# Layer A of a hybrid decoder trunk in the tokens' own order, with the convolved tiles of TensorE alone turned to phase order and back

## The chip, the cores and the metric

The kernel runs on one core of a Trainium2 chip. The metric is the device time of one execution in microseconds (us), the median of several runs. The engines are TensorE (PE: matmul and transpose), VectorE (DVE), ScalarE (ACT), GpSimd (POOL, hardly used here) and SyncE (SP, which issues all DMAs in one queue).

## What is computed

A trunk of two layers over x of 1024 tokens by 1024 channels, in float32. Layer A is a Conformer convolution, layer B a differential attention. The change touches layer A:

```
h = rms_norm(x, g_pre);  u = h @ w_in            # 1024 x 3072
a, b, z = split(u, 3)
c = a * sigmoid(b)
c = causal_depthwise_conv(c, w_dw) + b_dw        # 31 taps along the tokens
c = silu(layer_norm(c, ln_g, ln_b))              # over the channels
y = (c * silu(z)) @ w_out
x = x + rms_norm(y, g_post)
```

Layer B then computes K and V from x, eight heads of attention with two softmaxes each, a gated projection and a last normalised sum.

## The kernel before, in words

Everything is held with channels on the 128 partitions and tokens along the free dimension: 8 channel tiles c of 128, and 2 halves t of 512 tokens. Every matmul is done as three products of high and low fp32r parts (`THREE`), so each weight tile and each activation tile is split into a high part (a cast on ACT) and a low part (a subtraction on DVE): `wprep` for weights, `split` for activations. The activations of layer A's matmuls are `act[0]` and `act[1]`, one for each half.

The program is not in its written order. `Plan` collects operations with their data dependences, `schedule` simulates the engines with fixed costs and orders the operations by priorities, and `emit` writes the result out as a fixed order for each engine. The priorities come from the constants in `TUNE` and from an offset for each label in `OFFSETS`. On the chip each engine takes its instructions in that order and waits for data or for a buffer to come free. A `gate` binds only the plan's order.

Layer A before works in **phase order**: position s * 128 + n holds token 8 * n + s. The input is loaded in that order from a second copy of x, `xP`, that the host prepares. A "half" t of layer A's first part is then four phases, not 512 tokens that follow each other.

- `ab` (L835) computes, for a half and a channel tile, b and a: the product `pb_` times the RMS factor `rn[t]`, a tanh on ACT, then (tanh + 1) * `pa_` and a second DVE product with the RMS factor. For channel tiles of odd number the result goes to `cc` in phase order, contiguous (L858). For those of `DVC` = 0, 2, 4, 6 it is written in token order, with a stride of 8 elements (L847 to L855, two DVE instructions for each half).
- `conv` (L863) convolves. For tiles of `DVC`, 31 taps on DVE over 1024 tokens, the last of them reading with a stride of 8 so that `cb[t]` gets phase order (L873 to L879). For odd tiles, on TensorE: `cc` goes to DRAM, comes back as `xq` with 16 channels by 8 phases on the partitions, 80 matmuls follow, ACT adds the bias into `yq`, eight DMAs write `cv_d`, and two DMAs bring the result to `cb[0]` and `cb[1]` (L905).
- `zproj` (L916) projects z: 16 tiles of 24 matmuls each, for c = 0 to 4 both halves, then 5 to 7 of half 0 and of half 1. Its evacuations multiply by `rn[t]` and take SiLU into `sz[t]`. The buffers of `sz` take the space of the convolution's buffers (`wc`, `cc`, `xq`, `yq`, `ya`), so no `sz` is written before the last convolution is through with them.
- `lnorm` (L946) subtracts the mean, sums squares and spreads 1/std over the partitions by a matmul into a `pjB` PSUM tile. `rstd_bc` then copies that tile into `rn[t]`, the buffer that held the RMS factor of half t (L955). Then, for each c and each t: times 1/std, SiLU on ACT, times `sz`. A second loop (L966) splits to `act[t]`, which is wanted in token order: each half of tokens takes its elements from both `cb[0]` and `cb[1]`, with two casts on ACT and two subtractions on DVE of 128x256 for each tile, strided.
- `ymm` (L982) projects to y, 8 tiles of 24 matmuls for each half, which read `act[t]` from k = 0 to 7. `ypost` (L997) normalises, adds x and splits again for layer B.

PSUM: `pj` and `pjA` with 2 tiles each take the projections, `pjB` with 2 tiles the TensorE convolution, the means, the spread factors and half of y's tiles.

Of the kernel before, what the change touches and what calls it, by code (L numbers as in the profile page):

```python
# [13 lines left out]
ALU = mybir.AluOpType  # L14
# [4 lines left out]
P = 128  # L19
S = 1024  # L20
D = 1024
# [109 lines left out]
class Op:  # L131
# [16 lines left out]
TUNE = dict(LOOK=3.8682, BG=694967571912821345177968431443880025688058404755344259219980288,  # L148
           FS=45301, FS0=1201, CS=0, EV=157158, WT=0.6301, CV0=46679, CV1=113660, WP=2955,
           ZS=-61794, PT0=8, PT1=8)  # L150

OFFSETS = {"": 24050, "w": -5958, "start1": -20454, "x0": -59, "x1": -2750, "x2": 2563, "x3":
# [417 lines left out]
def trunk(ctx: ExitStack, tc, xT, xP, wC, prm, wA, wAo, wK, wV, wB, wBo, wBo2, gpost, outT, out2):  # L570
# [208 lines left out]
    def start_first():  # L779
# [3 lines left out]
        def load(k):  # L783
            R.dma(xh(k), xP[k * P : (k + 1) * P, :TH], 4 * P * TH)
# [33 lines left out]
    def start_second():  # L818
# [3 lines left out]
        for k in range(NT):  # L822
            R.dma(xh(k), xP[k * P : (k + 1) * P, TH:], 4 * P * TH)
# [638 lines left out]
```

## Time and profile before

| what | value |
|---|---|
| median of 3 runs | 1139.7 us (1139.49 to 1141.55) |
| the profiled execution's own time | 1131.87 us |
| its span, first to last instruction | 1130.0 us |
| mean granted TensorE clock | 0.984 |
| PE busy | 1070.5 us (95% of the span) |
| DVE busy | 918.9 us (81%) |
| ACT busy | 442.7 us (39%) |
| DMA | 121.31 MB, mean 107 GB/s |

The profile shows one execution, with every instruction's start and duration. It is read in three ways below: busy time of each engine in a stretch of the span, the waits of an engine with what ended them, and single instructions in order of time. The profiled execution is 7.8 us shorter than the median of the timed runs.

### The profile page before, as it was taken

Reading aid. Unit: us, or ns where it says so; the run is one execution under the profiler, and the core shown is the slowest. Engines: PE = TensorE matmul, PEld = TensorE weight load, DVE = VectorE, ACT = ScalarE, POOL = GpSimd, SP = SyncE. Lnnn points to the kernel's source line nnn. Section 1 sums busy time; section 2 is a strip of 40 time slices with the busy share of each in tenths; the row PEclk is TensorE's granted clock in tenths of the full one; section 3 lists DMA queues with packets and bytes.
Section 4 is the critical chain, followed back from the end, with each engine's and each line's share of the span. In section 5 each row is a group of like instructions: output and inputs, shape, how many; then the busy total and the mean of one; then the engine's idle time right before and its main releaser. Section 6 shows DMA issues by size and latency. Waiting matters only on the chain.

```text
span 1130.0 us, 15409 instructions
## 1 busy us (share of the span) xinstructions
PE 1070.5 (95%) x5790; PEld 877.1 (78%) x5790; DVE 918.9 (81%) x1828; ACT 442.7 (39%) x832; POOL 4.7 (0%) x19
## 2 busy tenths in 40 slices
PE   6999999999985999989999999999999999989896
PEld 4777878787863787877788877988779888767785
DVE  7999999999759379957878878788697877888657
ACT  8111020214356446434445334443344443455421
POOL 0000000000000000000000000000000000000000
PEclk9999999999996999999999999999999999999999
DMA  9121652523101245452013221141212311632564
GB/s 341 59 75 38 206 168 75 168 75 75 38 19 56 76 148 187 141 187 83 20 56 129 96 68 46 57 150 57 75 38 75 114 56 56 219 110 82 176 241 160
DMA packets 52985, 121.31 MB, mean 107 GB/s; under 512 B 5552, under 2 KB 22192, under 8 KB 51760
## 3 DMA queue, kind: packets, MB, share of 16 engines
q1 hardware_dynamic: 52912, 120.34, 31.2%
q8 instruction: 45, 0.74, 0.3%
q14 instruction: 28, 0.23, 0.1%
HBM read 90.96 MB, written 29.36 MB: 106 GB/s over the span
## 4 chain that ended last, share of the span: by engine, by line
PE 52%; DVE 9%; DMA 4%; issue 1%; ACT 1%; SPq 0%; DVEq 0%; ACTq 0%
PE pj L499 34%; PE o L499 6%; PE s L1171 5%; PE t L1223 3%; PE pjB L499 2%; DVE big L540 1%; DVE whl L540 1%; PE t L499 1%; DVE sm L540 1%; DMA outT<-tmp 1%; DMA wraw<-wBo 1%; PE pjA L499 1%; DMA x1t_d<-xr 1%; DMA tmp<-x_d 1%; DMA wraw<-wK 0%
## 5 line engine op out<-in xcount | busy, mean ns | idle before, releaser
L499 PE MATMUL pj<-act,whl 128*128 128x512 f32 x1968 | 532.1, 403 | 19.4 <-ACT whl L533 5.7
L499 PEld LDWEIGHTS pj<-act,whl 128*128 128x128 f32 x1968 | 354.9, 190 | 100.7 <-DVE act L540 7.3
L499 PE MATMUL pjA<-act,whl 128*128 128x512 f32 x672 | 183.7, 399 | 2.2 <-DVE sz L540 1.2
L499 PEld LDWEIGHTS pjA<-act,whl 128*128 128x128 f32 x672 | 125.0, 188 | 33.9 <-DVE sz L540 1.7
L560 DVE SCALAR_TENSOR_TENSOR ya<-cc,pr,ya 128x1024 f32<-128x1024 f32 x116 | 148.6, 1281 | 2.7
L522 ACT ACTIVATE e<-e,sm 128x128 f32<-128x128 f32 (+7 forms) x128 | 99.2, 776 | 91.5 <-DVE sm L1180 47.7
L533 ACT CAST whl<-wraw 128x1024 fp32r<-128x1024 f32 (+1 forms) x84 | 85.9, 1027 | 101.3 <-PE pj L499 71.3
L540 DVE TENSOR_TENSOR whl<-wraw,whl 128x1024 fp32r<-128x1024 f32 (+1 forms) x84 | 99.9, 1194 | 14.7 <-ACT whl L533 14.6
L499 PE MATMUL pj<-whl,act 128*128 128x256 f32 x768 | 111.4, 284 | 0.5 <-DVE tmp L560 0.4
L499 PEld LDWEIGHTS pj<-whl,act 128*128 128x128 f32 x768 | 99.6, 188 | 3.6 <-DVE tmp L560 1.1
L499 PE MATMUL o<-at,vt 128*128 128x256 f32 x480 | 100.2, 299 | 2.3 <-DVE at L540 1.7
L1180 DVE CUSTOM_DVE_ANT_0 e<-s,dist 128x128 f32<-128x128 f32 (+7 forms) x128 | 94.5, 752 | 6.5 <-PE s L1171 4.3
L499 PEld LDWEIGHTS o<-at,vt 128*128 128x128 f32 x480 | 78.1, 189 | 16.9 <-issue 3.0
L540 DVE TENSOR_TENSOR at<-t,at 128x512 fp32r<-128x512 f32 (+1 forms) x80 | 50.7, 634 | 29.1 <-ACT at L533 28.6
L1171 PE MATMUL s<-ks,qs 64*128 64x512 f32 (+2 forms) x576 | 72.6, 372 | 0.3 <-DVE sm L1180 0.3
L533 ACT CAST at<-t 128x512 fp32r<-128x512 f32 (+1 forms) x80 | 43.4, 542 | 70.2 <-PE t L1223 69.1
L1171 PEld LDWEIGHTS s<-ks,qs 64*128 64x128 f32 x576 | 48.1, 187 | 20.7 <-issue 8.4
L499 PE MATMUL pjB<-act,whl 128*128 128x512 f32 x192 | 52.9, 404 | 11.3 <-ACT act L533 8.3
L560 DVE SCALAR_TENSOR_TENSOR e<-e,sm,e 128x128 f32<-128x128 f32 (+3 forms) x64 | 52.2, 817 | 1.5
L499 PEld LDWEIGHTS pjB<-act,whl 128*128 128x128 f32 x192 | 36.7, 192 | 21.0 <-ACT act L533 8.7
L1223 PE MATMUL t<-ident,e 128*128 128x128 f32 x288 | 50.5, 275 | 0.8 <-DVE og L540 0.8
L540 DVE TENSOR_TENSOR tmp<-pj,rn 128x512 f32<-128x512 f32 x48 | 32.7, 685 | 14.3 <-PE pj L499 9.2
(176 smaller groups left out, 1093.2 us busy)
## 6 DMA issues: line engine op xcount, KB each, us to landing
wraw<-wA SPq DMA_DIRECT2D x22, 512.0 KB, 3.5
wc<-wC SPq DMA_DIRECT2D x8, 1280.0 KB, 7.9
wraw<-wAo SPq DMA_DIRECT2D x16, 512.0 KB, 3.5
wraw<-wB SPq DMA_DIRECT2D x16, 512.0 KB, 3.4
v_d<-tmp SPq DMA_DIRECT2D x32, 256.0 KB, 2.5
vt<-v_d SPq DMA_DIRECT2D x16, 512.0 KB, 3.7
wraw<-wBo SPq DMA_DIRECT2D x16, 512.0 KB, 3.9
go_d<-fx SPq DMA_DIRECT2D x12, 512.0 KB, 2.6
```

Source lines behind the costliest of these rows:

```text
L499: e.matmul(w[0], lhsT=r[2 * i], rhs=r[2 * i + 1], start=start and i == 0, stop=stop and i == k - 1)
L522: e.activation(w[0], r[0], func, **kw)
L533: (e.copy if hasattr(e, "activation") else e.tensor_copy)(w[0], r[0])
L540: lambda e, r, w: e.tensor_tensor(w[0], r[0], r[1], alu), [a, b], [out])
L560: e.scalar_tensor_tensor(w[0], r[0], s if imm else r[2], r[1], o1, o2)
L1171: en.matmul(w_[2 * (m // 6) + m % 2], lhsT=r[2 * m], rhs=r[2 * m + 1], start=m % 6 < 2, stop=m % 6 >= 4)
L1180: en.tensor_tensor_reduce(w_[0], r[0], r[1], -(0.5 ** (h + 1)), 3e38, ALU.add, ALU.min, w_[1])
L1223: R.op([("PE", 110.0)], lambda en, r, w: en.transpose(w[0], r[0], ident), [aw[qq][:, k0 : k0 + P]], [t_ps[:, i, :]])
```

## The change

- x is loaded from `xT` in token order; `xP` is gone. A half is now 512 tokens that follow each other, all through layer A.
- `ab` multiplies (tanh + 1) by the RMS factor first, SBUF by SBUF, and then by `pa_`. For tiles of `DVC` the second product is written contiguously. For odd tiles it reads both operands with a stride of 8 elements and writes phase order for TensorE.
- `conv`: the last DVE tap is a plain instruction for each half. For odd tiles one DMA brings the whole convolved tile to a buffer `yb` (in the slots of `xq`), and two ScalarE copies of 128x512, reading with a stride, turn it to token order in `cb[0]` and `cb[1]`.
- `lnorm`: 1/std of half t goes to a `msum` buffer and no longer to `rn[t]`. The loop runs over half 0 with all its channel tiles and then over half 1, and each tile is split at once by `split`, one cast and one subtraction of 128x512, contiguous.
- The constants of the plan (`LOOK`, `BG`, `WT`) and all its offsets are new, so the written order of the whole kernel is redrawn. The code of layer B is the same.

```
-TUNE = dict(LOOK=3.8682, BG=694967571912821345177968431443880025688058404755344259219980288,
-           FS=45301, FS0=1201, CS=0, EV=157158, WT=0.6301, CV0=46679, CV1=113660, WP=2955,
+TUNE = dict(LOOK=2.2803,
+           BG=19323277573972505648901158565292249389628248258332383962132468097051787264,
+           FS=45301, FS0=1201, CS=0, EV=157158, WT=0.8342, CV0=46679, CV1=113660, WP=2955,
            ZS=-61794, PT0=8, PT1=8)
...
-            R.dma(xh(k), xP[k * P : (k + 1) * P, :TH], 4 * P * TH)
+            R.dma(xh(k), xT[k * P : (k + 1) * P, :TH], 4 * P * TH)
...
         pa_ = R.tile("pjA", TH)
         proj(pa_.all(), ha, act[t])
+        R.stt(sg.all(), sg.all(), 1.0, rb.all(), ALU.add, ALU.mult)
         if c in DVC:
-            o = cc[:, 32:].rearrange("p (n s) -> p s n", s=PH)._then(
-                lambda ap: ap[:, PH // 2 * t : PH // 2 * (t + 1)])
-            ph = "p (s n) -> p s n"
-            R.op([("DVE", 700.0)], lambda e, r, w: e.scalar_tensor_tensor(
-                w[0], r[0], 1.0, r[1], ALU.add, ALU.mult),
-                [sg.all().rearrange(ph, s=PH // 2), pa_.all().rearrange(ph, s=PH // 2)], [o])
-            if rb is not None:
-                R.op([("DVE", 700.0)], lambda e, r, w: e.tensor_tensor(
-                    w[0], r[0], r[1], ALU.mult), [o, rb.all().rearrange(ph, s=PH // 2)], [o])
+            R.tt(cc[:, 32 + t * TH : 32 + (t + 1) * TH], sg.all(), pa_.all(), ALU.mult)
             return
-        o = cc[:, t * TH : (t + 1) * TH]
-        R.stt(o, sg.all(), 1.0, pa_.all(), ALU.add, ALU.mult)
-        if rb is not None:
-            R.tt(o, o, rb.all(), ALU.mult)
+        ph = lambda v: v.all().rearrange("p (n s) -> p s n", s=PH)
+        o = cc[:, :S].rearrange("p (s n) -> p s n", s=PH)._then(
+            lambda ap: ap[:, :, P // 2 * t : P // 2 * (t + 1)])
+        R.op([("DVE", 1200.0)], lambda e, r, w: e.tensor_tensor(w[0], r[0], r[1], ALU.mult),
+             [ph(sg), ph(pa_)], [o])
...
             for t in range(2):
-                nat = lambda v: v.rearrange("p (n s) -> p s n", s=PH)._then(
-                    lambda ap, t=t: ap[:, PH // 2 * t : PH // 2 * (t + 1)])
-                R.op([("DVE", 720.0)], lambda e, r, w: e.scalar_tensor_tensor(
-                    w[0], r[0], r[2], r[1], ALU.mult, ALU.add),
-                    [nat(src(KW - 1)), nat(y.all()), tap(KW - 1)],
-                    [cb[t][:, c, :].rearrange("p (s n) -> p s n", s=PH // 2)])
+                R.stt(cb[t][:, c, :], src(KW - 1, t), tap(KW - 1),
+                      y[:, t * TH : (t + 1) * TH], ALU.mult, ALU.add)
...
+        yb = R.tile("xq", S, lane="Y")
+        R.dma(yb.all(), cv_d[c], 4 * P * S)
         for t in range(2):
-            R.dma(cb[t][:, c, :], cv_d[c, :, t * TH : (t + 1) * TH], 4 * P * TH)
+            src = yb.all().rearrange("p (s n) -> p n s", s=PH)._then(
+                lambda ap, t=t: ap[:, P // 2 * t : P // 2 * (t + 1)])
+            R.copy(cb[t][:, c, :].rearrange("p (n s) -> p n s", s=PH), src).alts = [("ACT", 1000.0)]
...
-            rb[t] = rstd_bc(sq_sum(t, lambda k: cb[t][:, k, :]), "dg0", "pjB", rn[t])
-        for c in range(NT):
-            for t in range(2):
+            rb[t] = rstd_bc(sq_sum(t, lambda k: cb[t][:, k, :]), "dg0", "pjB",
+                            R.tile("msum", TH))
+        for t in range(2):
+            for c in range(NT):
                 R.label = f"ln{t}{c}"
...
                 R.act(v, v, AF.Silu, scale=col(C_LNG, c), bias=col(C_LNB, c))
                 R.tt(v, v, sz[t][:, c, :], ALU.mult)
-
-        for t in range(2):
-            for c in range(NT):
                 R.label = f"sp{t}{c}"
-                for x in range(2):
-                    dst = act[t][:, c, x, :].rearrange("p (n s) -> p s n", s=PH)
...
+                split(act[t], c, v)
```

## Rows read from the trace of the kernel before

**Rows 1.** The view of windows, one row for each stretch of the span. Columns: the stretch and its length in us; busy time and, in brackets, instructions of PE, PEld, DVE, ACT and POOL; the granted TensorE clock (1.00 is 2.4 GHz); the DMA engines' mean busy share; GB/s.

```profile
0.00:28.00 28.00, 18.91 (x72) 13.88 (x73) 21.52 (x37) 22.93 (x39) 1.15 (x12) 1.00 0.92 343
28.00:262.00 234.00, 226.66 (x1134) 186.76 (x1132) 229.12 (x247) 38.19 (x69) 0.63 (x5) 1.00 0.34 109
...
289.00:325.00 36.00, 36.00 (x159) 29.08 (x158) 19.60 (x41) 11.27 (x18) 0.00 (x0) 1.00 0.09 30
325.00:335.00 10.00, 9.79 (x42) 7.54 (x41) 9.26 (x15) 9.77 (x17) 0.00 (x0) 1.00 0.00 0
335.00:360.00 25.00, 8.71 (x19) 5.80 (x20) 24.23 (x41) 19.53 (x34) 0.00 (x0) 0.66 0.21 63
...
440.00:520.00 80.00, 72.56 (x421) 60.41 (x420) 59.51 (x129) 31.66 (x58) 2.95 (x2) 0.98 0.43 144
520.00:1000.00 480.00, 477.24 (x2912) 396.30 (x2911) 387.29 (x956) 208.93 (x438) 0.00 (x0) 1.00 0.24 84
1000.00:1130.00 130.00, 114.89 (x584) 93.04 (x582) 92.77 (x240) 47.72 (x85) 0.00 (x0) 0.95 0.43 150
```

**Rows 2.** The view of waits for TensorE between 330 and 370 us: engine and line that waited, what ended the wait, total us, how often, the longest.

```profile
PE pjB L499 <- ACT act L533: 8.3, 1, 8.3
PE pj L499 <- DVE act L540: 5.6, 2, 5.1
PE pjB L499 <- DVE act L540: 3.0, 1, 3.0
```

**Rows 3.** The timeline of TensorE from 334 to 361 us (start, us, what, how many, and in square brackets the idle time before with what ended it): the end of the last tile of z and the first matmul of y.

```profile
333.69 1.09 PE L499 MATMUL pj<-act,whl 128*128 128x512 f32 x4
343.07 0.80 PE L499 MATMUL pjB<-act,whl 128*128 128x512 f32 x1 [8.29 <-ACT act L533]
```

**Rows 4.** The chain of waits, one piece of TensorE at full clock in y's stage.

```profile
390.55 4.20 PE pj L499 x18
```

**Rows 5.** The timeline of TensorE from 286 to 312 us: the two matmul pairs that spread 1/std over the partitions (the first for half 0, the second for half 1).

```profile
287.85 0.62 PE L499 MATMUL pjB<-dg,ones_r 128*128 128x512 f32 x2
...
310.37 0.62 PE L499 MATMUL pjB<-dg,ones_r 128*128 128x512 f32 x2
```

**Rows 6.** The timeline of VectorE from 318 to 326 us: z's evacuations and the first product with 1/std.

```profile
318.72 0.69 DVE L540 TENSOR_TENSOR sz<-pjA,rn 128x512 f32<-128x512 f32 x1 [6.78 <-PE pjA L499]
322.92 0.69 DVE L540 TENSOR_TENSOR sz<-pj,rn 128x512 f32<-128x512 f32 x1 [3.51 <-PE pj L499]
323.62 0.69 DVE L540 TENSOR_TENSOR sz<-pjA,rn 128x512 f32<-128x512 f32 x1
324.97 1.30 DVE L540 TENSOR_TENSOR big<-big,rn 128x512 f32<-128x512 f32 x2 [0.65 <-ACT rn L533]
```

**Rows 7.** The timeline of ScalarE from 322 to 326 us: the copy of 1/std of half 0 into `rn`.

```profile
324.35 0.59 ACT L533 COPY rn<-pjB 128x512 f32<-128x512 f32 x1
```

**Rows 8.** Groups of instructions by line and form between 320 and 372 us (count, then busy us and mean ns of one, then idle time before): the LayerNorm's products, SiLU and split.

```profile
L540 DVE TENSOR_TENSOR act<-big,act 128x256 fp32r<-128x256 f32 x32 | 18.5, 651 | 0.0
L533 ACT CAST act<-big 128x256 fp32r<-128x256 f32 x32 | 18.2, 698 | 6.7 <-DVE big L540 6.7
L522 ACT ACTIVATE big<-big,pr 128x512 f32<-128x512 f32 x16 | 12.3, 800 | 2.9 <-DVE big L540 2.9
L540 DVE TENSOR_TENSOR big<-big,sz 128x512 f32<-128x512 f32 x16 | 10.9, 690 | 1.1 <-ACT big L522 0.7 <-ACT sz L522 0.3
L540 DVE TENSOR_TENSOR big<-big,rn 128x512 f32<-128x512 f32 x16 | 10.7, 689 | 0.7 <-ACT rn L533 0.7
```

**Rows 9.** The same view from 0 to 400 us: `ab`'s products (strided at L854 and L850, contiguous at L540 and L560), the last tap (L876) and a contiguous product with a column scalar.

```profile
L560 DVE SCALAR_TENSOR_TENSOR act<-big,pr,act 128x512 fp32r<-128x512 f32 x16 | 11.5, 741 | 5.3 <-ACT act L522 5.3
...
L854 DVE TENSOR_TENSOR cc<-cc,rn 128x512 f32<-128x512 f32 x8 | 10.1, 1268 | 0.2
...
L876 DVE SCALAR_TENSOR_TENSOR big<-cc,pr,ya 128x512 f32<-128x512 f32 x8 | 9.9, 1270 | 0.1
L850 DVE SCALAR_TENSOR_TENSOR cc<-tmp,pjA 128x512 f32<-128x512 f32 x8 | 9.4, 1169 | 0.7 <-ACT tmp L522 0.7
...
L540 DVE TENSOR_TENSOR cc<-cc,rn 128x512 f32<-128x512 f32 x8 | 5.5, 681 | 0.0
L560 DVE SCALAR_TENSOR_TENSOR cc<-tmp,pjA 128x512 f32<-128x512 f32 x8 | 5.4, 677 | 0.0
```

**Rows 10.** The view of waits for TensorE between 28 and 262 us.

```profile
PE pj L499 <- DVE tmp L540: 5.0, 3, 2.5
PE pjA L499 <- DVE cc L850: 0.9, 1, 0.9
```

**Rows 11.** The timeline of all engines from 222 to 286 us: the last convolved tile of TensorE on its way to `cb`, and TensorE's wait behind it.

```profile
251.21 2.26 ACT L522 ACTIVATE yq<-pjB,pr 128x128 f32<-128x128 f32 x8 [19.97 <-PE pjB L499]
...
253.50 3.63 SPq L565 DMA_DIRECT2D cv_d<-yq  x8
...
257.29 1.92 SPq L565 DMA_DIRECT2D big<-cv_d  x2
...
262.62 1.67 PE L499 MATMUL pjA<-act,whl 128*128 128x512 f32 x6 [1.24 <-DVE sz L540]
```

**Rows 12.** The groups of ScalarE between 28 and 262 us: the weights' casts and `ab`'s tanh.

```profile
L533 ACT CAST whl<-wraw 128x1024 fp32r<-128x1024 f32 x18 | 18.8, 1049 | 58.7 <-PE pj L499 43.3 <-PE pjA L499 8.4 <-issue 7.1
L522 ACT ACTIVATE tmp<-tmp 128x512 f32<-128x512 f32 x16 | 10.1, 633 | 57.8 <-DVE tmp L540 57.8
```

More of the change, by code (lines that the diff above doesn't have):

```diff
@@ L144 @@
            ("SP", "POOL"): 940.0, ("SP", "SP"): 1000.0}
-TUNE = dict(LOOK=3.8682, BG=694967571912821345177968431443880025688058404755344259219980288,
-           FS=45301, FS0=1201, CS=0, EV=157158, WT=0.6301, CV0=46679, CV1=113660, WP=2955,
+TUNE = dict(LOOK=2.2803,
+           BG=19323277573972505648901158565292249389628248258332383962132468097051787264,
+           FS=45301, FS0=1201, CS=0, EV=157158, WT=0.8342, CV0=46679, CV1=113660, WP=2955,
            ZS=-61794, PT0=8, PT1=8)
-OFFSETS = {"": 24050, "w": -5958, "start1": -20454, "x0": -59, "x1": -2750, "x2": 2563, "x3":
[57 rows of a table removed]
+OFFSETS = {"": 20890, "w": 8673, "start1": -150, "x0": 332, "x1": 403, "x2": 60, "x3": 48533,
[55 rows of a table added]
 class Clock:
@@ L569, in trunk @@
 @with_exitstack
-def trunk(ctx: ExitStack, tc, xT, xP, wC, prm, wA, wAo, wK, wV, wB, wBo, wBo2, gpost, outT, out2):
+def trunk(ctx: ExitStack, tc, xT, wC, prm, wA, wAo, wK, wV, wB, wBo, wBo2, gpost, outT, out2):
     nc = tc.nc
@@ L822, in start_second @@
         for k in range(NT):
-            R.dma(xh(k), xP[k * P : (k + 1) * P, TH:], 4 * P * TH)
+            R.dma(xh(k), xT[k * P : (k + 1) * P, TH:], 4 * P * TH)
         for k in range(NT):
@@ L867, in conv @@
             tap = lambda j: col(C_TAP, (KW + 1) * DVC.index(c) + j)
-            src = lambda j: cc[:, 2 + j : 2 + j + S]
+            src = lambda j, t=None: (cc[:, 2 + j : 2 + j + S] if t is None else
+                                     cc[:, 2 + j + t * TH : 2 + j + (t + 1) * TH])
             y = R.tile("ya", S)
@@ L964, in lnorm @@
                 R.tt(v, v, sz[t][:, c, :], ALU.mult)
-        for t in range(2):
-            for c in range(NT):
                 R.label = f"sp{t}{c}"
-                for x in range(2):
-                    dst = act[t][:, c, x, :].rearrange("p (n s) -> p s n", s=PH)
-                    for u in range(2):
-                        src = cb[u][:, c, :].rearrange("p (s n) -> p s n", s=PH // 2)._then(
-                            lambda ap, t=t: ap[:, :, 64 * t : 64 * t + 64])
-                        d = dst._then(lambda ap, u=u: ap[:, 4 * u : 4 * u + 4])
-                        if x == 0:
-                            R.copy(d, src).alts = [("ACT", 306.0)]
-                        else:
-                            hi = f(act[t][:, c, 0, :]).rearrange("p (n s) -> p s n", s=PH)._then(
-                                lambda ap, u=u: ap[:, 4 * u : 4 * u + 4])
-                            R.tt(d, src, hi, ALU.subtract).alts = [("DVE", 336.0)]
+                split(act[t], c, v)
     def ymm(t):
@@ L1436 @@
         "xT": np.ascontiguousarray(np.asarray(x)[0].T),
-        "xP": np.ascontiguousarray(
-            np.asarray(x)[0].T.reshape(D, S // PH, PH).transpose(0, 2, 1).reshape(D, S)),
         "wC": np.ascontiguousarray(wc.reshape(NT * (NT // GB), P, GB * SH * P)),
```

112 rows, old and new, of the table OFFSETS are left out of this document.

## The prediction

> **What bounds the kernel now.** I read the windows by stage first [rows 1]. TensorE is busy in 95% of the span, and the reader should look for where it is not. From 520 to 1000 us, the attention, it misses 2.8 of 480 us; from 28 to 262, the projections and convolutions of layer A, 7.3 of 234; from 440 to 520, the passage to layer B, 7.4; at the two ends 9.1 and 15.1. One place stands out: from 335 to 360 us only 19 matmuls touch a stretch of 25 us, with the granted clock down to 0.66 as a mean of its two levels, while VectorE is busy for 24.2 of them and ScalarE for 19.5. Next I asked what TensorE waits for there: `act`, first its cast, then its subtractions [rows 2]. The timeline shows z's last matmuls at 333.7 to 334.8 and y's first at 343.07 after 8.29 us of nothing [rows 3]. So the LayerNorm between z and y bounds this stage, and TensorE bounds nearly everything else. The other stretch to read is 28 to 262, where VectorE is busy for 229.1 of 234 us: there the two engines are close to a tie.
>
> Why is the LayerNorm late? Its factor 1/std for half 0 was spread into PSUM at 287.85 [rows 5], but the first product with it starts at 324.97 [rows 6]. In between stands the copy of that factor into `rn[0]`, at 324.35 [rows 7]. `rn[0]` still held the RMS factor that z's evacuations of half 0 read, and the last of those starts at 323.62 [rows 6]. For 36 us the factor lay ready behind a buffer. VectorE was meanwhile busy for 19.6 of the 36 us from 289 to 325, ScalarE for 11.3 [rows 1]. Then both halves came at once, and `act[0]` needs elements of both, so TensorE had to wait for nearly all of it.
>
> **Term 1, the hole after z.** The change puts 1/std into a `msum` buffer whose last reader is the mean's matmul, and splits half 0 from half 0 alone. Half 0 then costs VectorE 8 x (0.69 + 0.69) for the two products and 8 x 0.68 for a contiguous subtraction, 16.5 us, and ScalarE 8 x 0.80 for SiLU and 8 x 0.59 for the cast, 11.1 us [rows 7 to 9]. Idle time before 325 is 16.4 us on VectorE and 24.7 on ScalarE [rows 1], and the ten us to 335 were already spent on this work. The last tile needs the z evacuated at 323.62; with SiLU of it (0.63, as for the tanh of the same form [rows 12]), product, cast and subtraction (0.69, 0.59, 0.68) it is ready near 327, and y reads it last of eight. So y can start when z ends. What comes back is 25.0 us less the time of 19 matmuls at the full rate of 4.20 / 18 = 0.233 us [rows 4], 4.4 us: 20.6, and 0.2 from 325 to 335 [rows 1]. **-20.8 us.** Next in line is half 1: another 16.5 us of VectorE under the 8 x 24 x 0.233 = 45 us that y's half 0 takes, so nothing is late there. The split also falls from 18.5 to 16 x 0.68 = 10.9 us on VectorE and from 18.2 to 9.4 us on ScalarE [rows 7 to 9]; under that cover it is worth nothing more.
>
> **Term 2, the gates and taps on VectorE.** The strided forms cost 9.4 + 10.1 + 9.9 = 29.4 us at L850, L854 and L876. Contiguous they are two groups of 8 x 0.68 and one of 8 x 0.74, 16.8 us [rows 9]. Against that, the eight last products of the odd tiles now read both operands with a stride, one of them PSUM. No row shows a strided read of PSUM. Nearest is L876, two strided reads from SBUF with a contiguous write, 1.27 us; the contiguous 0.68 is the lower bound, and 2.5 (two such steps) my upper one. I take 1.27: 8 x 0.59 = 4.7 us more. Net relief 12.6 - 4.7 = 7.9 us, with bounds 12.6 and -2.0. What is it worth? TensorE waited for VectorE for only 5.9 us there [rows 10], and 1.24 behind it [rows 11], so at most 7.1; losing 2.0 us of VectorE at a tie costs at most 2. VectorE's load falls by 3.4%, so I take a third of its waits. **-2 us.**
>
> Of the stride the Trainium skill says otherwise: VectorE: DVE Perf Modes, section "Mode 1× (REGULAR) — the baseline", has that mode take "fp32, weird strides, PSUM operands" at one result a cycle. By it the strided forms would cost what the contiguous ones do, the relief would be 0, and the time 1120.9. The trace disagrees: 1.17 to 1.27 us against 0.68 for the same 512 elements [rows 9], and the measurement decides.
>
> **Term 3, the way of the convolved tile.** One load takes the place of two, and two ScalarE copies of 128x512 follow. A contiguous copy is 0.59 us [rows 7]; the strided casts of 128x256 have 0.70 [rows 8], 1.4 for 512. I take 1.0 each, between the two. Eight of them are 8 us of ScalarE in a stretch where it idles for 196 of 234 [rows 1]. For the first three odd tiles only the mean's sum waits. For the last one `sz` waits, since it lies in the convolution's buffers, and before TensorE stood for 1.24 us at that place [rows 11], so there is no cover: **+2 us**, with bounds 0 and 2.8. The sent-off DMAs are one fewer for each odd tile; loading x from `xT` moves the same bytes. Both at nothing: the order in SP's queue is otherwise kept.
>
> **Term 4, the redrawn order.** Layer B's code is the same but its order is new. Outside 28 to 440 us TensorE idles for 34.4 us [rows 1]; I let a quarter of it, 8.6 us, come or go, and take **0**.
>
> Sum: -20.8 - 2 + 2 + 0 = -20.8 us. On the profiled execution's own 1131.87 us (span 1130.0) this gives 1111.1. The timed runs' median stands 7.8 us higher, and I carry that over: 1139.7 - 20.8 = **1118.9 us**.
>
> **Rivals.**
> - The relief pays in full: all 7.1 us of waits at the tie go, and the copies cost nothing. 1139.7 - 20.8 - 7.1 = 1111.8. For it: VectorE is at 98% there [rows 1]. Against: TensorE is at 97% itself.
> - Part of the hole stays: the new order lets half 1's statistics and z's evacuations go ahead of half 0 on VectorE, or the first weights of y wait behind SiLU on ScalarE. With half of it left, 1139.7 - 10.4 = 1129.3. For it: ScalarE is busy for 9.8 of the 10 us before 335 [rows 1]. Against: the idle time counted above.
> - The change doesn't do what it says: another buffer or the plan's order holds half 0 until z ends. 1139.7. Against: the second spread is through by 311 [rows 5], and nothing else stands on `msum`.
> - Slower: ScalarE stands at its new copies. They wait for eight writes and a read through DRAM; from the last `yq` to the last load's issue it was 5.7 us before [rows 11]. Behind them in ScalarE's queue are the casts of weights and the tanh of the next gates [rows 12], for which VectorE and then TensorE wait. TensorE has cover of one channel tile's two halves, 48 x 0.233 = 11.2 us. Each odd tile that holds ScalarE for longer costs the excess, four times: 16.4 us each would eat all of term 1, and 18 us give 1139.7 - 20.8 + 27 = 1146. Against: the order would have to place the copies far ahead of the data.
>
> **How the numbers follow.** Forecast 62%, own range 1110 to 1127.5 by term 4; relief in full 10%; half of the hole 14%, give or take 4 us; no effect 5%; slower 9%. The range 1109.5 to 1131 takes in the forecast, the relief and two thirds of the half hole, 81%. A measurement of this kernel can tell some 0.2%, 2.3 us, from no change. Faster: 62 + 10 + 14 + 1 = 87%; same 4%; slower 9%.
>
> **What would show it.** Term 1: no wait of TensorE for `act` over 2 us between z and y, clock at 1.00 throughout, the first product with 1/std before z's last evacuation of half 0. Term 2: the strided product near 1.27 us, contiguous ones at 0.68, and VectorE's waits in the convolution's stretch below 6 us. Term 3: copies near 1.0 us and a wait at z's first evacuation of up to 3 us. Term 4: layer B's idle time between 25 and 43 us. I am wrong if a wait for `act` of 10 us remains, or if ScalarE's idle time before the copies holds up the tanh.

## The result and the profile after

| | before | after |
|---|---|---|
| median of the runs side by side | 1139.6 us (1136.99 to 1141.55) | 1125.29 us (1123.27 to 1127.16) |
| span of the profiled execution | 1130.0 us | 1125.4 us |
| PE / DVE / ACT busy | 1070.5 / 918.9 / 442.7 us | 1074.9 / 899.9 / 445.6 us |
| mean granted TensorE clock | 0.984 | 0.981 |

The ratio is 0.9877, interval 0.9852 to 0.9902: 14.3 us faster. The forecast was 20.8 us and the time is within the range. A second profile of each (the two repeats below) has spans of 1138.4 and 1121.1 us. So the short execution of before on which the working rests was one execution's luck, and the 7.8 us added to reach the median were rightly added.

The windows of the changed kernel, with the columns of [rows 1]:

```profile
28.00:262.00 234.00, 226.47 (x1123) 188.86 (x1123) 215.62 (x244) 43.99 (x75) 0.62 (x5) 0.98 0.35 109
262.00:289.00 27.00, 21.80 (x88) 16.66 (x88) 23.22 (x45) 11.63 (x17) 0.00 (x0) 0.87 0.12 39
289.00:325.00 36.00, 36.00 (x158) 28.84 (x157) 33.63 (x67) 22.31 (x33) 0.00 (x0) 1.00 0.08 30
325.00:335.00 10.00, 10.00 (x44) 8.07 (x43) 9.45 (x15) 7.27 (x12) 0.00 (x0) 1.00 0.31 107
335.00:360.00 25.00, 25.00 (x108) 20.13 (x108) 15.56 (x21) 12.57 (x19) 0.00 (x0) 1.00 0.19 62
440.00:520.00 80.00, 73.22 (x422) 60.30 (x422) 56.54 (x123) 33.41 (x63) 2.86 (x2) 0.96 0.40 138
520.00:1000.00 480.00, 475.82 (x2903) 396.01 (x2902) 386.31 (x962) 206.29 (x429) 0.00 (x0) 0.99 0.24 84
1000.00:1125.00 125.00, 108.71 (x547) 87.80 (x545) 85.01 (x214) 45.88 (x81) 0.00 (x0) 0.95 0.43 152
```

From 335 to 360 us TensorE now does 108 matmuls in 25.00 of 25 us at a clock of 1.00, where it did 19 in 8.71 [rows 1]. VectorE is busy for 33.6 of the 36 us before 325 instead of 19.6: the LayerNorm's products went into its idle time. But 262 to 289 has a new hole: 5.2 us idle, and a clock of 0.87. The waits of TensorE up to 300 us, as the view lists them (who waits <- for whom, us in total, times, longest):

```profile
PE pjB L498 <- DMA xq<-ca_d: 6.4, 2, 5.0
PE pj L498 <- ACT whl L532: 5.7, 1, 5.7
PE pjB L498 <- DVE msum L539: 5.2, 1, 5.2
```

The waits for `tmp` and `cc` of [rows 10] are gone. In their place stand one for the gathers of a tile's phases from DRAM and one for the mean's sum (the one for `whl` is at the start). Where they stand, in TensorE's timeline, with the windows of the same places below:

```profile
135.13 2.47 PE L498 MATMUL pjB<-xq,wc 128*128 128x128 f32 x10 [5.00 <-DMA xq<-ca_d]
...
239.07 1.35 PE L498 MATMUL pjB<-xq,wc 128*128 128x128 f32 x10 [1.35 <-DMA xq<-ca_d]
...
269.54 2.04 PE L498 MATMUL pjB<-msum,ones_r 128*128 128x512 f32 x2 [5.20 <-DVE msum L539]
```

```profile
135.00:140.00 5.00, 4.87 (x20) 4.61 (x21) 4.86 (x5) 0.00 (x0) 0.00 (x0) 0.50 0.00 0
140.00:145.00 5.00, 5.00 (x40) 4.87 (x40) 4.89 (x5) 0.00 (x0) 0.00 (x0) 0.94 0.02 3
265.00:270.00 5.00, 0.46 (x1) 0.49 (x2) 5.00 (x9) 0.18 (x1) 0.00 (x0) 0.69 0.30 105
270.00:275.00 5.00, 5.00 (x13) 3.20 (x13) 5.00 (x9) 4.25 (x7) 0.00 (x0) 0.62 0.01 3
```

Each wait costs more than its length: the clock is 0.50 (the lower of its two levels, 1.2 GHz) from 135 to 140 us and 0.62 on the mean from 270 to 275, with TensorE busy.

So the account is kept in **lost time**: idle time of TensorE plus its busy time x (1 - granted clock), summed over windows of 5 us, the last one shorter. For the two profiles of each kernel, in us:

| stretch | before | before again | after | after again | change of the mean |
|---|---|---|---|---|---|
| 0 to 30 | 9.5 | 8.7 | 8.2 | 8.4 | -0.8 |
| 30 to 240 | 6.3 | 9.3 | 10.8 | 11.2 | +3.2 |
| 240 to 280, the convolution's end | 1.3 | 1.2 | 7.2 | 7.0 | +5.9 |
| 280 to 420, z to y | 21.1 | 21.2 | 0 | 0 | -21.1 |
| 420 to 515 | 8.9 | 10.8 | 13.0 | 9.9 | +1.6 |
| 515 to 1000 | 4.1 | 4.7 | 7.4 | 8.9 | +3.8 |
| 1000 to the end | 16.9 | 19.9 | 18.3 | 16.6 | -1.0 |

The sum is -8.5 us, and the means of the spans differ by 10.9; the other 2.4 us are in the work itself, as the profile counts it at full clock. Two executions of one kernel differ by up to 3 us in a stretch and 8 in the span, so only the third and fourth rows say much by themselves. The second does not: two runs below that keep the order of before in that stretch lose 12.0 and 11.1 us there, and up to 2.5 us of the row are a low clock from 30 to 35 us, which only the first profile of before lacks. What is shown of it are its parts: the waits for the gates, 5.9 us, are gone, and the new wait at 135 us costs 5.0 us and 2.8 us of slow clock behind it.

VectorE shows how the two new holes hang together. These are its timeline after 28 us at its longest wait, and the convolution's last tap with what follows it; the second fence has the last tap of before:

```profile
152.53 1.29 DVE L539 TENSOR_TENSOR tmp<-pj,rn 128x512 f32<-128x512 f32 x2 [7.23 <-PE pj L498]
...
266.18 1.40 DVE L559 SCALAR_TENSOR_TENSOR big<-cc,pr,ya 128x512 f32<-128x512 f32 x2
267.51 2.49 DVE L539 TENSOR_TENSOR msum<-msum,big 128x512 f32<-128x512 f32 x4
269.91 0.68 DVE L539 TENSOR_TENSOR sz<-pjA,rn 128x512 f32<-128x512 f32 x1
```

```profile
259.26 2.42 DVE L876 SCALAR_TENSOR_TENSOR big<-cc,pr,ya 128x512 f32<-128x512 f32 x2
```

From 28 us to the end of its last tap VectorE worked 7.8 us less than before (221.2 against 229.0), and yet that tap ended at 267.6 us, where it had ended at 261.7, because it stood idle for 18.4 us instead of 4.7. (The 13.5 us between the two windows of 28 to 262 are more than that, since part of the work only moved behind 262.) TensorE, late from 135 us, came late with the next `pj`, and VectorE stood for 7.2 us, 9.8 with its shorter waits for `pj`; it is the engine that ends the convolution. The other part is the mean's sum, which can't end until the turned tiles are there. TensorE's wait bears the sum's name, but z's first evacuation stands right behind the same additions, at 269.91 us, so without the mean's matmul TensorE would have waited for `sz` until about the same time. SP's and ScalarE's timelines near the end of the convolution:

```profile
241.96 0.43 SPq L564 DMA_DIRECT2D xq<-cv_d  x1
...
248.05 2.67 SPq L564 DMA_DIRECT2D xq<-cv_d  x2
...
257.14 0.34 SPq L564 DMA_DIRECT2D xq<-cv_d  x1
```

```profile
245.94 2.09 ACT L532 COPY big<-xq 128x512 f32<-128x512 f32 x2 [13.34 <-DMA xq<-cv_d]
...
251.45 4.33 ACT L532 COPY big<-xq 128x512 f32<-128x512 f32 x4
...
260.56 2.19 ACT L532 COPY big<-xq 128x512 f32<-128x512 f32 x2 [4.78 <-DMA xq<-cv_d]
```

All four odd tiles come back between 242 and 263 us, though the first was written out by 130. `yb` takes a slot of `xq`, of which there are two, and the order had already given both to the gathers of later tiles: GpSimd clears their 32 border columns long ahead.

```profile
116.19 0.12 POOL L874 MEMSET xq<- 128x32 f32 x1 [39.03 <-PE pjB L498]
...
148.35 0.12 POOL L874 MEMSET xq<- 128x32 f32 x1 [22.27 <-PE pjB L498]
```

### The profile page after: what moved, and what is told of

Its sections match the earlier page's. It is cut to its first block, busy times and chain, and to the rows that moved or that the text cites. A ratio compares the mean times of both kernels' runs of the same rounds, so it can differ in the third digit from the quotient of the medians.

```text
span 1125.4 us, 15385 instructions
## 1 busy us (share of the span) xinstructions
PE 1074.9 (96%) x5790; PEld 883.0 (78%) x5790; DVE 899.9 (80%) x1812; ACT 445.6 (40%) x824; POOL 4.8 (0%) x19
## 4 chain that ended last, share of the span: by engine, by line
PE 79%; DVE 8%; DMA 7%; ACT 3%; issue 2%; SPq 1%; DVEq 0%; ACTq 0%
PE pj L498 45%; PE pjA L498 11%; PE pjB L498 6%; PE o L498 6%; PE s L1152 6%; PE t L1204 3%; DMA wc<-wC 2%; PE pjC L498 1%; DMA wraw<-wBo 1%; SPq L564 1%; DVE ya L559 1%; PE t L498 1%; DMA wraw<-wK 1%; ACT tmp L521 1%; DVE msum L539 1%
## 5 line engine op out<-in xcount | busy, mean ns | idle before, releaser
L498 PE MATMUL pjA<-act,whl 128*128 128x512 f32 x672 | 186.8, 402 | 0.6 <-DVE whl L539 0.6
L498 PEld LDWEIGHTS pjA<-act,whl 128*128 128x128 f32 x672 | 127.3, 191 | 32.0 <-DVE whl L539 1.0
L498 PEld LDWEIGHTS pjB<-xq,wc 128*128 128x128 f32 x320 | 39.8, 200 | 8.3 <-issue 7.2
```

The costliest lines, as they stand in the source:

```text
L498: e.matmul(w[0], lhsT=r[2 * i], rhs=r[2 * i + 1], start=start and i == 0, stop=stop and i == k - 1)
```

## The experiments

Theory A: the hole after z was `rn[t]`'s alone, it is filled, and what is missing from the forecast was lost in the convolution: tiles that came back late through shared buffers, and gathers late behind writes. Rival B: the missing part is the redrawn order of layer B. Rival C: the hole was filled by the split in halves or by the new constants, not by the buffer. The first four runs below shared one chip; the run with y's weights cast earlier and the last two shared another; the other four a third. Each ratio is to before on its own chip (medians 1140.18, 1139.07, 1139.08 us).

**Code and constants apart.** The first run is the changed code with the constants of before, the second the code of before with the changed constants.

```diff
 # first: after.py
-TUNE, OFFSETS = those of after
+TUNE, OFFSETS = those of before
 # second: before.py
-TUNE, OFFSETS = those of before
+TUNE, OFFSETS = those of after
```

> The changed code with the constants and offsets of the kernel before. If the code (1/std in its own buffer, halves apart) filled the hole after z: no wait of TensorE for act over 2 us between z and y, and about 1139.6 - 20.6 = 1119 us, give or take 10 because the constants were not drawn for this code. If the gain came from the new constants alone: at or above 1135 us, with a wait for act of some 8 us after z.

Measured: 1138.24 us (1134.34 to 1143.13), ratio 0.999 (0.9969 to 1.0012). The time is what was expected if the constants had done it, the waits are those expected of the code: the hole after z is filled here too, and 330 to 420 us lose 2.5 us. The gain is given away elsewhere: 420 to 515 us lose 20.8 us instead of 8.9 to 10.8, and 240 to 280 lose 14.9 instead of 1.3, most of it in one wait, in TensorE's timeline of this run:

```profile
270.63 1.65 PE L499 MATMUL pjA<-act,whl 128*128 128x512 f32 x3 [12.91 <-DVE sz L540]
```

From 30 to 240 us this run loses only 3.7 us, with no wait for the gates. But its last tap on VectorE ends at 269.8 us, later still than in the changed kernel, and z's first evacuation comes behind it.

> The code before with the changed kernel's constants and offsets. If the code filled the hole: a hole of about 20 us after z remains and the time is 1135 us or more. If the constants did it: no wait for act over 3 us there and about 1125 us.

Measured: 1181.14 us (1173.96 to 1181.31), ratio 1.0347 (1.0309 to 1.0385). The hole stays, in TensorE's timeline of this run:

```profile
367.95 0.79 PE L498 MATMUL pj<-act,whl 128*128 128x512 f32 x1 [20.08 <-ACT act L532]
```

So the code fills the hole and the constants don't. But an order drawn with the other code's constants costs 13 us with the new code (1138.2 against 1125.3) and 41 with the old.

**1/std back in `rn[t]`**, everything else as changed, halves included.

```diff
-            rb[t] = rstd_bc(sq_sum(t, lambda k: cb[t][:, k, :]), "dg0", "pjB",
-                            R.tile("msum", TH))
+            rb[t] = rstd_bc(sq_sum(t, lambda k: cb[t][:, k, :]), "dg0", "pjB", rn[t])
```

> The changed kernel with 1/std copied to rn[t] again, as before, the halves still apart. If the buffer that z still reads was the cause: the first product with 1/std starts only after z's last evacuation of half 0, TensorE waits for act after z, and the kernel is 8 to 15 us slower than the changed one (1133 to 1140). If the halves are what counts: half 0 alone is ready soon after z, the wait is under 4 us and the time within 4 us of 1125.

Measured: 1161.05 us (1159.69 to 1161.45), ratio 1.0187 (1.0158 to 1.0216). That is outside the 1133 to 1140 us expected. The hole is back and longer: 27.2 us lost from 330 to 420. VectorE's first products with 1/std, the cast of y's first weights on ScalarE and TensorE's wait, from their timelines in this run:

```profile
340.16 1.90 DVE L539 TENSOR_TENSOR big<-big,rn 128x512 f32<-128x512 f32 x3
...
364.48 1.03 ACT L532 CAST whl<-wraw 128x1024 fp32r<-128x1024 f32 x1
...
365.56 1.22 PE L498 MATMUL pj<-act,whl 128*128 128x512 f32 x2 [22.59 <-ACT whl L532]
```

In the changed kernel the first product with 1/std stands at 293.53. Here the copy into `rn` goes at 339.54 us, behind z's evacuations of half 0, and the product behind it, as expected: the buffer holds half 0 until z has all but ended, halves apart or not. But not all of the 22.59 us is the buffer's. The plan redrew the order for this run, and the wait ended with weights whose cast stands behind SiLU and casts of both halves on ScalarE; seven of the eight subtractions of the half that came first were through by 353.5 us, the eighth by 358.9. Rival C falls in so far as the halves alone don't remove the wait; how far they shorten it this run doesn't show, as up to 12 us of it are the order's. (Of some 21 us over before, 6 are the longer hole and 5 the convolution's end as in the changed kernel; some 11 lie past 1000 us, where 30.0 us are lost against 17 to 20.)

**The buffer alone.** Before with 1/std in `msum`, first with the plan left to redraw its order, then with each engine's order given as a list: that of before, with only the LayerNorm's products, SiLU, splits and the copy of 1/std moved forward into idle time.

```diff
-            rb[t] = rstd_bc(sq_sum(t, lambda k: cb[t][:, k, :]), "dg0", "pjB", rn[t])
+            rb[t] = rstd_bc(sq_sum(t, lambda k: cb[t][:, k, :]), "dg0", "pjB",
+                            R.tile("msum", TH))
 # second run: schedule() follows a list; labels ln.. and sp.. moved forward in it
```

> The kernel before with one edit: 1/std goes to a msum buffer; phase order, the loops over both halves and all constants as before. If the buffer was the cause: the first product with 1/std starts well before 320 us, the hole of 20.6 us shrinks to under 8 us, and the time is 1120 to 1128 us. If the halves are what counts: the wait for act stays above 10 us, since act[0] still needs both halves, and the time is 1134 to 1140.

Measured: 1180.05 us (1176.17 to 1183.21), ratio 1.0351 (1.0317 to 1.0385). The hole shrinks to 8.8 us lost, but layer B loses 88 us from 420 on, where before loses 30 to 35. One line moved no work of layer B; the plan's new order of it did this.

> The kernel before with 1/std in a msum buffer, as in the run before, but the order no longer redrawn: every engine keeps the order of the kernel before, and only the LayerNorm's products, SiLU, splits and the two copies of 1/std move forward to idle time. If the buffer was the cause of the hole and the redrawn order the cause of the 40 us that the run before lost: the stretch from z's end to y loses under 8 us of TensorE instead of 20.6, all other stages lose what they lost before, and the time is 1120 to 1128 us. If phase order and the joined halves keep act[0] late: a wait of 10 us or more for act stays and the time is 1133 or more.

Measured: 1128.2 us (1125.94 to 1130.36), ratio 0.9902 (0.9871 to 0.9933). With the order held, the buffer alone is worth 10.9 us. 9.9 us stay lost from 330 to 420, where under 8 were expected, in TensorE's timeline of this run:

```profile
341.67 0.79 PE L558 MATMUL pjB<-act,whl 128*128 128x512 f32 x2 [2.67 <-ACT whl L592]
344.54 0.80 PE L558 MATMUL pjB<-act,whl 128*128 128x512 f32 x1 [2.07 <-DVE whl L599]
348.32 1.22 PE L558 MATMUL pj<-act,whl 128*128 128x512 f32 x2 [1.71 <-ACT whl L592]
```

and the window of 340 to 345 us of this run and, below it, of the changed kernel:

```profile
340.00:345.00 5.00, 1.25 (x3) 0.76 (x4) 5.00 (x7) 5.00 (x11) 0.00 (x0) 0.72 0.17 53
```

```profile
340.00:345.00 5.00, 5.00 (x23) 4.05 (x22) 3.74 (x6) 3.41 (x6) 0.00 (x0) 1.00 0.00 0
```

VectorE and ScalarE are both full here (5.00 of 5 us each), ScalarE with strided casts of both halves and the weights of y among them; in the changed kernel 3.74 and 3.41 us are busy.

**Is it only the place of y's first weights?** The same kernel with the casts of y's first two weight tiles about 10 us earlier; some of the LayerNorm's operations shift around them.

```diff
 # the lists of ACT and DVE, on top of the last run
+whl<-wraw (y00w, y01w): right behind the slots that z's tiles 15 and 16 free
```

> The kernel before in its own order with 1/std in a msum buffer and the LayerNorm moved forward, as in the earlier run, and y's first two weight tiles cast some 10 us earlier, before ScalarE's strided casts. If ScalarE's queue, not the joined halves' data, left 9.9 us of hole there: it falls under 5 us and the time is 1122 to 1125. If act[0] itself is late because it needs both halves: the wait for weights becomes a wait for act and the time stays within 2 us of 1128.

Measured: 1129.1 us (1128.7 to 1129.94), ratio 0.9911 (0.9897 to 0.9924), nothing gained. The waits moved on to the next weight tiles, and 330 to 365 us lose 10.1 us:

```profile
340.92 0.74 PE L558 MATMUL pjB<-act,whl 128*128 128x512 f32 x2 [2.23 <-ACT whl L592]
...
347.65 1.22 PE L558 MATMUL pj<-act,whl 128*128 128x512 f32 x2 [4.20 <-ACT whl L592]
```

So it was not the place of those two casts alone. But the waits did not become waits for `act` either: each still ends with weights whose cast stands behind strided casts in ScalarE's queue. That the whole stretch is too full is argued from the windows, and whether a better order on ScalarE would do is open. That the split by halves is what relieves it was not tried alone, as it can't be had in phase order: there each half of tokens takes its elements from both tiles.

**Two repeats**, of before (a single execution) and of the changed kernel.

```diff
 (no change)
```

> The kernel before once more, for a second profile. If its first profiled execution (1131.87 us against a median of 1140) was a lucky one in its granted clock: this one is nearer to 1140, with more time at the lower clock level outside the hole after z, and the same waits. If the profiler always shortens it: again about 1132.

Measured: 1140.17 us with a profile, span 1138.4. Its waits stand where the first profile's stand; its lost time is in the table above. So the profiler does not always shorten the execution.

> The changed kernel once more, as a neighbour for the other runs and for a second profile: 1123 to 1127 us, no wait of TensorE for act after z, and the same 5 us waits near 135 and 269 us.

Measured: 1125.33 us (1122.85 to 1128.57), ratio 0.9887 (0.9851 to 0.9922). TensorE waits again 4.95 us at 134.52 for the gathers and 5.22 at 269.50 for the mean's sum.

**The tiles back earlier.** The changed kernel with loads, copies and mean sums of tiles 1 and 3 at 130 to 200 us, and the clearing of `xq` for tiles 5 and 7 behind them.

```diff
 # the lists of SP, ACT, DVE and POOL
-memset xq (tiles 5, 7) at 116 and 148 us; xq<-cv_d, big<-xq x2, msum (tiles 1, 3) from 242 us
+xq<-cv_d, big<-xq x2, msum (tiles 1, 3) at 130 to 200 us; memset xq (tiles 5, 7) behind them
```

> The changed kernel in its own order, with one thing moved: the loads, ScalarE copies and mean sums of convolved tiles 1 and 3 (and the sums of 2 and 4) come when their data is there, about 130 to 200 us, and not after 242 us; the memsets of the input buffers of tiles 5 and 7, which held both slots, come after them. If the crowding of copies and sums at the end of the convolution made TensorE's 5.2 us wait for the mean: that wait falls under 2 us, the stretch from 240 to 280 us loses under 3 us instead of 7.2, and the kernel is 4 to 6 us faster than the changed one. If the taps of VectorE alone set that time: the wait stays within 1.5 us of 5.2 and the time within 2 us of the changed kernel.

Measured: 1122.91 us (1121.43 to 1127.11), ratio 0.9862 (0.9835 to 0.989): 2.4 us less than the repeat on the same chip, about half of what A expected, and the two intervals overlap. The mean's wait falls from 5.22 to 3.79 us, and 240 to 280 lose 5.1 us instead of 7.0. Two new waits of VectorE stand in this run, from its timeline:

```profile
147.99 0.69 DVE L597 TENSOR_TENSOR msum<-big 128x512 f32<-128x512 f32 x1 [4.60 <-ACT big L590]
...
262.71 1.23 DVE L597 TENSOR_TENSOR whl<-wraw,whl 128x1024 fp32r<-128x1024 f32 x1 [5.27 <-ACT whl L590]
```

The second one is the slower rival's mechanism in small: ScalarE stands for 6.88 us at tile 7's copies, with a cast of weights behind them in its queue, and VectorE waits for that cast.

**Gathers ahead of writes.** The changed kernel with one exchange in SP's queue.

```diff
 # SP's list, near 117 us
-cv_d<-yq x8 (tile 1), xq<-ca_d x8 (tile 3)
+xq<-ca_d x8 (tile 3), cv_d<-yq x8 (tile 1)
```

> The changed kernel in its own order, with one thing moved on SP's queue: the eight gathers of convolved tile 3 stand ahead of the eight writes of tile 1, and no longer behind them. If the place in SP's queue made TensorE's 5.0 us wait near 135 us and the slow clock after it: that wait goes to under 1 us, the stretch from 30 to 240 us loses 4 to 7 us less, and the kernel is 4 to 7 us faster than the changed one, unless the wait for the mean at 269 us, which hangs on VectorE's taps, grows by the same. If VectorE sets the end of the convolution: the wait at 135 goes, the one at 269 grows to 9 to 12 us, and the time is within 2 us of 1125.

Measured: 1119.45 us (1114.63 to 1123.58), ratio 0.9822 (0.9795 to 0.9848), some 5.9 us below the changed kernel's two medians of 1125.3 from runs beside other ones of before (whose medians agree within 1.2 us); the runs spread over 9 us, and the profiled execution (1122.56 us) is no shorter than the repeat's (1122.85). SP's timeline of the changed kernel and then of this run, with TensorE's wait in this run as the third fence:

```profile
117.33 11.93 SPq L564 DMA_DIRECT2D cv_d<-yq  x8
129.33 3.72 SPq L564 DMA_DIRECT2D xq<-ca_d  x8
```

```profile
125.53 5.54 SPq L622 DMA_DIRECT2D xq<-ca_d  x8
131.18 3.69 SPq L622 DMA_DIRECT2D cv_d<-yq  x8
```

```profile
133.09 2.47 PE L556 MATMUL pjB<-xq,wc 128*128 128x128 f32 x10 [2.84 <-DMA cv_d<-yq]
```

The gathers go out 3.8 us earlier, the wait falls from 5.00 to 2.84 us (under 1 was expected; the view names the writes, though the matmul reads `xq`), 30 to 240 us lose 7.2 us instead of 10.8 to 11.2, and VectorE's wait at 149 us falls from 7.23 to 3.84. The last tap ends at 264.7 instead of 267.6 us. The wait for the mean's sum is as long as ever (5.38), and 240 to 280 us lose 8.1 us: it is the other cause. About 3 us of the gain are traced to this place; in the rest of the span the differences are no larger than between two executions.

Why the gathers could not go at once: they read what the write of tile 3, `ca_d<-cc`, leaves in DRAM. SP issued it at 115.47 us in the changed kernel, between two loads of convolution weights of 1280 KB each, and GpSimd, which clears `cc` behind it, had to wait until 125.96:

```profile
125.96 0.12 POOL L1062 MEMSET cc<- 128x32 f32 x1 [9.65 <-DMA ca_d<-cc]
```

In this run SP stood 8.9 us at the head of the gathers for the same write. So SP's order cost the changed kernel's gathers some 3.8 us, and the rest of their delay is the write's late landing, which no run took away.

**Both moves together.**

```diff
 # both edits of lists above
```

> Both moves together: tile 1's and 3's copies and mean sums early, and tile 3's gathers first. If both waits are the new order's own: 1125.3 - 2.4 - 4 to 7 = 1116 to 1119 us. If VectorE sets the end of the convolution: 1122 to 1124, as with the first move alone.

Measured: 1118.33 us (1116.01 to 1120.0), ratio 0.9814 (0.9798 to 0.983). That is within the 1116 to 1119 us expected. TensorE's waits are shorter but not gone: 2.4 us at the gathers and 3.9 for the mean's sum. The last tap ends at 263.5, and 240 to 280 lose 5.4 us. VectorE waits again for a cast of weights behind tile 7's copies, for whose load ScalarE stood 6.97 us:

```profile
260.98 1.23 DVE L597 TENSOR_TENSOR whl<-wraw,whl 128x1024 fp32r<-128x1024 f32 x1 [5.38 <-ACT whl L590]
```

It is the fastest of all, 7 us below the changed kernel. Over the gathers alone the 1.1 us are within the runs' spread; against the early tiles alone, from which it differs only by the exchange, it gains 4.6 us. So the exchange gave 5.9 and 4.6 us, the early tiles 2.4 and 1.1.

The order of the four versions by the end of the last tap is the order of their medians (not of the profiled executions, of which that of the gathers alone is longer than that of the early tiles): 267.6 us (1125.3), 265.3 (1122.9), 264.7 (1119.5), 263.5 (1118.3).

## Why the prediction was right, and where it was not

**Term 1 was right**, in place, cause and size: 21.1 us of lost time went where 20.8 were forecast. TensorE waits for nothing between z and y, the first product with 1/std stands at 293.53 and the first with `sz` at 306.07, and the clock is 1.00:

```profile
293.53 0.69 DVE L539 TENSOR_TENSOR big<-big,msum 128x512 f32<-128x512 f32 x1 [0.32 <-ACT msum L532]
```

1/std back in `rn[t]` brings the hole back, and the buffer alone, in the old order, takes 10.9 us of it. Here the prediction was too coarse: it gave the whole to the buffer and called the split worth nothing more. With both halves in one run and strided casts, 9.9 us stay lost, in waits for weights behind a full ScalarE. That the halves and the plain casts empty it is argued from the windows, not tried alone.

**Term 2 was right on the instructions and wrong on what they are worth.** The strided product and the contiguous one, from the groups of VectorE between 28 and 280 us, with ScalarE's new copies:

```profile
L852 DVE TENSOR_TENSOR cc<-tmp,pjA 128x512 f32<-128x512 f32 x8 | 9.1, 1133 | 0.0
...
L539 DVE TENSOR_TENSOR cc<-tmp,pjA 128x512 f32<-128x512 f32 x8 | 5.4, 682 | 0.1
```

```profile
L532 ACT COPY big<-xq 128x512 f32<-128x512 f32 x8 | 8.6, 1138 | 18.1 <-DMA xq<-cv_d 18.1
```

1.13 us against 1.27 estimated, and waits of TensorE for the gates from 5.9 us to none. The rule of the Trainium skill's VectorE: DVE Perf Modes, "Mode 1× (REGULAR) — the baseline", which takes strides at one result a cycle, disagrees with this too: the same shape takes 1133 ns with the stride and 682 without. VectorE's work up to the last tap fell by 7.8 us, where 7.9 were forecast; that they agree so well is partly chance, since sums and subtractions for weights moved across that tap too. But 13.7 us more of idle time came with it, and the expected 2 us were not to be had: VectorE's waits were to stay below 6 us, and those for `pj` alone took 9.8. A shorter load on VectorE pays only if nothing else holds up its last tap; the changed code with the old constants shows it too, with no wait for the gates and the latest last tap.

**Term 3 is the step that failed.** It priced instructions: the copies are 1.14 us each against 1.0. It took the rest at nothing, "the order in SP's queue is otherwise kept", and for the first three odd tiles "only the mean's sum waits". The two places cost 5.9 us at 240 to 280 and, less the waits for the gates that went, some 3 at 30 to 240, where +2 was forecast with 2.8 as the upper bound. The wait at z's first evacuation, to be up to 3 us, is 5.2. First, SP's order was not kept: the writes of tile 1 keep the gathers of tile 3 back until 129.3 us, and TensorE reaches its matmuls at 130.1 us. Before, the gathers went out at 127.4, but TensorE did not come to them until 133.7, as SP's and TensorE's timelines of before have it:

```profile
127.42 3.61 SPq L565 DMA_DIRECT2D xq<-ca_d  x8
...
133.70 9.09 PE L499 MATMUL pjB<-xq,wc 128*128 128x128 f32 x80
```

Exchanging writes and gathers gave back 5.9 and 4.6 us in two comparisons, about 3 of them traced; the landing of tile 3's write at some 126 us, which the sum did not price either, allows no more there. Second, `yb` in `xq`'s slots could not come early, so every odd tile came late, and the mean's sum, which the prediction named as waiting but not as waited for, had 14 additions on VectorE between 247 and 270 us, among the last taps. Moving two tiles forward took 1.4 us off that wait. What is left of it, 3.9 us with both moves, stands behind VectorE's wait for a cast that follows tile 7's copies; no run took that away.

**Term 4** held as a bound and fell short as a place. From 420 us on, the mean lost time rose by 4.4 us (+1.6, +3.8, -1.0), within the 8.6 allowed, and no run isolates it: rival B stands for a part of that size at most. The two runs that keep before's order and have the buffer alone lose 37.0 and 34.5 us there, where before loses 29.9 and 35.4 and the changed kernel 38.7 and 35.4, so the rise is no larger than what executions of one order differ by. But the prediction let the redrawn order act only outside 28 to 440 us. Its larger price, the places of gathers and loads, was inside. With constants not drawn for the code the order alone cost 13 to 41 us.

**The rivals.** The relief in full did not come; the hole did not stay by half; the change does what it says. The slower rival, ScalarE at its copies, is there, but twice and shorter: 13.34 us at 245.94 and 4.78 at 260.56, and not 16 us four times; of the rival's cover of 11.2 us only the first exceeds it, by 2.1. With the two places eased the kernel runs at 1118.3 us, where the forecast of 1118.9 lay; that they agree so closely is partly chance, since term 4 and the relief differ from their forecasts too.

## What to carry to other kernels

Look for a factor that is ready long before its first use and ask whose last read holds its buffer; price the filled hole by the matmuls that are missing in it. When a change adds a round trip through shared buffers and in-order queues, price the place of each load and not the length of the copy: who holds the slots, what is ahead in the queue, and when the waiting engine gets there. And measure an edit in a planned kernel with the order held, or the plan's redraw will be taken for the edit.

## What was not expected of the hardware

A wait of TensorE of about 5 us is followed by a lower clock: 0.50 from 135 to 140 us after one of 5.00 us, 0.62 from 270 to 275 after one of 5.20, which adds some 2 to 3 us of lost time to each. The strided product that reads PSUM (1.13 us) is no dearer than the nearest one that reads SBUF only (1.27 for L876, another operation [rows 9]). A ScalarE copy of 128x512 that reads with a stride takes 1.14 us, a contiguous one, from PSUM, 0.59 [rows 7]. Executions of before on one chip run from 1135 to 1145 us, so 2 us can't be read from one profile.
